# Log-sum-exp of 16384 rows on one core: one-pass row sums on VectorE, the last three sums in PSUM, most logs ahead of the last load

## The chip, the core and the metric

One core of one Trainium2 chip. The metric is the device time of one execution in microseconds (us). The profile's span is about 1.9 us shorter than that time (161.4 against 163.31 before). ScalarE is ACT in the profile, VectorE is DVE, SP is the engine that issues the loads.

## The reference

```python
def setup_inputs():
    batch, seq, dim = 32, 512, 1024
    return {"x": np.random.randn(batch, seq, dim).astype(np.float32), "axis": -1}

def reference(x, axis):
    x_max = np.max(x, axis=axis, keepdims=True)
    return (x_max.squeeze(axis) + np.log(np.sum(np.exp(x - x_max), axis=axis))).astype(np.float32)
```

The kernels take exp without subtracting the maximum, and were found correct in every run below.

## The kernel before

Each of the 128 partitions holds 128 rows of 1024 numbers. They come in 17 loads, into a ring of 51 rows. Per load, `(r, n_dve)` says: r rows, of which ScalarE takes the exp of the first `n_dve` in one instruction and VectorE sums them; of the others ScalarE takes exp and sum in one instruction per row. "A row" below is such a row on all partitions, 0.524 MB.

```python
CHUNKS = [
    (4, 1), (15, 11), (16, 10), (16, 15), (16, 0), (14, 0), (12, 9), (9, 5), (7, 5), (5, 4),
    (4, 3), (3, 0), (2, 2), (2, 2), (1, 0), (1, 0), (1, 0),
]
LN_AT = 5
# ... cut: ring, sums, res in SBUF; a semaphore per load; load(i) waits until its ring rows are free
    for i, (r, n_dve) in enumerate(CHUNKS):
        if i:
            load(i)
        s, row = place[i]
        if i == LN_AT:
            logged = row
            take_logs(0, logged, *done_before[i])      # waits for all sums of the loads before
        nc.scalar.wait_ge(landed[i], 16)
        if n_dve:
            nc.scalar.activation(out=ring[:, s : s + n_dve], in_=ring[:, s : s + n_dve],
                                 func=Exp).then_inc(act_done, 1)
            acts += 1
            nc.vector.wait_ge(act_done, acts)
            nc.vector.reduce_sum(out=sums[:, row : row + n_dve], in_=ring[:, s : s + n_dve],
                                 axis=AX).then_inc(dve_done, 1)
            # ... cut: bookkeeping
        for j in range(n_dve, r):
            nc.scalar.activation(out=ring[:, s + j], in_=ring[:, s + j], func=Exp,
                                 accum_out=sums[:, row + j : row + j + 1]).then_inc(act_done, 1)
            # ... cut
    take_logs(logged, NB, dves, acts)
    nc.scalar.dma_start(out=out_v, in_=res).then_inc(stored, 16)
```

The softmax here doesn't subtract the row's maximum and nothing guards it: scores larger than these inputs give would overflow.

## Time and profile before

| | before |
|---|---|
| time, median of 6 runs | 163.32 us (163.15 to 164.0) |
| span of the profiled run | 161.4 us |
| input queue's share of 16 DMA engines | 97.0% |
| last row landed / its exp started | 158.21 / 158.34 |

### The profile page before, as it was taken

To read this page: it belongs to the slowest core of one execution; us is meant where nothing else is said; L and a number is where in the kernel's file an instruction comes from. 1 tells how busy PE (TensorE), PEld (TensorE's weight loads), DVE (VectorE), ACT (ScalarE), POOL (GpSimd) and SP (SyncE) were. 2 spreads that over 40 slices of the span, in tenths; PEclk is the share of its full clock that TensorE was granted. 3 is DMA by queue.
4 is the path that set the end of the run, shared out by engine and by line. 5 is a ranking of instruction groups with operands and counts; after the bars stand their busy time and mean duration, and the time that the engine had idled before them with its cause. 6 is when DMAs were issued, how large, how long until landed. Compare 5 with 4: busy or idle time off the path is not lost.

```text
span 161.4 us, 212 instructions
## 1 busy us (share of the span) xinstructions
DVE 72.9 (45%) x11; ACT 124.1 (77%) x136; POOL 0.2 (0%) x4
## 2 busy tenths in 40 slices
DVE  0030000029960699000799920000004999799874
ACT  3190006997089980999429999999999999999995
POOL 0000000000000000000000000000000000000000
DMA  7999799989989989989989999999899999999990
GB/s 264 499 487 442 335 442 520 422 357 520 422 357 520 422 357 520 422 357 520 422 353 426 457 455 422 390 463 475 347 439 434 433 441 402 431 418 416 420 394 24
DMA packets 2593, 67.18 MB, mean 416 GB/s; under 512 B 288, under 2 KB 416, under 8 KB 800
## 3 DMA queue, kind: packets, MB, share of 16 engines
q1 hardware_dynamic: 2448, 67.11, 97.0%
q10 hardware_dynamic: 144, 0.07, 0.1%
q14 instruction: 1, 0.01, 0.0%
HBM read 67.11 MB, written 0.07 MB: 416 GB/s over the span
## 4 chain that ended last, share of the span: by engine, by line
ACT 52%; DMA 38%; DVE 7%; issue 1%
DMA ring<-in_x_dram 38%; ACT ring L127 30%; ACT ring L115 22%; DVE sums L120 7%; ACT res L92 0%
## 5 line engine op out<-in xcount | busy, mean ns | idle before, releaser
L120 DVE TENSOR_REDUCE sums<-ring 128x5 f32<-128x5120 f32 (+8 forms) x11 | 72.9, 6648 | 86.1 <-ACT ring L115 86.0
L115 ACT ACTIVATE ring<-ring 128x5120 f32<-128x5120 f32 (+8 forms) x11 | 59.3, 5395 | 29.6 <-DMA ring<-in_x_dram 29.6
L127 ACT ACTIVATE ring<-ring 128x1024 f32<-128x1024 f32 x61 | 63.4, 1041 | 5.3 <-DMA ring<-in_x_dram 5.3
L127 ACT ACTIVATION_READ_ACCUMULATOR ring<-ring 128x1 f32 x61 | 11.4, 187 | 0.0
L102 ACT ACT_TABLE_LOAD x1 | 1.3, 1283 | 0.8 <-PEq L181 0.8
L92 ACT ACTIVATE res<-sums 128x67 f32<-128x67 f32 (+1 forms) x2 | 0.5, 256 | 0.1
L181 POOL MEMSET const-bfloat16-1.0<- 128x1 bf16 x1 | 0.1, 101 | 0.0
L181 POOL MEMSET const-uint8-127<- 128x1 uint8 x1 | 0.1, 101 | 0.0
L181 POOL MEMSET const-float32-0.0<- 128x1 f32 x1 | 0.1, 98 | 0.2 <-issue 0.2
L181 POOL MEMSET const-float32-1.0<- 128x1 f32 x1 | 0.1, 98 | 0.0
## 6 DMA issues: line engine op xcount, KB each, us to landing
ring<-in_x_dram SPq DMA_DIRECT2D x1, 7680.0 KB, 24.9
ring<-in_x_dram SPq DMA_DIRECT2D x1, 7168.0 KB, 36.0
ring<-in_x_dram SPq DMA_DIRECT2D x1, 6144.0 KB, 21.6
ring<-in_x_dram SPq DMA_DIRECT2D x1, 4608.0 KB, 32.1
ring<-in_x_dram SPq DMA_DIRECT2D x2, 2048.0 KB, 26.3
ring<-in_x_dram SPq DMA_DIRECT2D x1, 3584.0 KB, 40.2
ring<-in_x_dram SPq DMA_DIRECT2D x1, 2560.0 KB, 44.4
ring<-in_x_dram SPq DMA_DIRECT2D x2, 1024.0 KB, 46.0
```

What stands on the lines that cost most here:

```text
L92: nc.scalar.activation(out=res[:, lo:hi], in_=sums[:, lo:hi], func=Ln).then_inc(act_done, 1)
L102: nc.scalar.preload_act_table_set("natural_log_exp_and_others")
L115: nc.scalar.activation(out=ring[:, s : s + n_dve], in_=ring[:, s : s + n_dve], func=Exp).then_inc(act_done, 1)
L120: nc.vector.reduce_sum(out=sums[:, row : row + n_dve], in_=ring[:, s : s + n_dve], axis=AX).then_inc(dve_done, 1)
L127: nc.scalar.activation(out=ring[:, s + j], in_=ring[:, s + j], func=Exp, accum_out=sums[:, row + j : row + j + 1],).then_inc(act_done, 1)
L181: nc = _bacc.Bacc("TRN2", target_bir_lowering=False, num_devices=1)
```

## The change

The intent: sum a row on VectorE in one pass of 512 columns, adding its two halves and accumulating (`tensor_tensor_reduce`), in place of a reduce over 1024; give VectorE 96 rows instead of 67; keep the sums of the last three rows in PSUM; and take all other logs before the last row, while ScalarE waits for it, so that only a log of three columns is left behind the last exp.

```diff
 CHUNKS = [
-    (4, 1), (15, 11), (16, 10), (16, 15), (16, 0), (14, 0), (12, 9), (9, 5), (7, 5), (5, 4),
-    (4, 3), (3, 0), (2, 2), (2, 2), (1, 0), (1, 0), (1, 0),
+    (4, 4), (15, 13), (15, 14), (16, 9), (16, 11), (16, 11), (12, 7), (9, 9), (7, 6),
+    (5, 3), (4, 3), (3, 3), (2, 2), (1, 1), (1, 0), (1, 0), (1, 0),
 ]
-LN_AT = 5
+LN_AT = 7
+LATE = 3
 # ... cut
+    late = nc.alloc_psum_tensor("late", [P, 512], fp32).ap()
 # ... cut: take_logs gets its source; total(t) is late[...] for the last three rows, else sums[...]
+        if i == len(CHUNKS) - 1:
+            take_logs(logged, late_row, sums[:, logged:late_row], *done_before[-LATE])
         nc.scalar.wait_ge(landed[i], 16)
 # ... cut
-            nc.vector.reduce_sum(
-                out=sums[:, row : row + n_dve], in_=ring[:, s : s + n_dve], axis=AX
-            ).then_inc(dve_done, 1)
+            for j in range(n_dve):
+                nc.vector.tensor_tensor_reduce(
+                    out=ring[:, s + j, : D // 2],
+                    in0=ring[:, s + j, : D // 2], in1=ring[:, s + j, D // 2 :],
+                    scale=1.0, scalar=0.0, op0=Add, op1=Add,
+                    accum_out=sums[:, row + j : row + j + 1],
+                ).then_inc(dve_done, 1)
 # ... cut
-                accum_out=sums[:, row + j : row + j + 1],
+                accum_out=total(row + j),
 # ... cut
-    take_logs(logged, NB, dves, acts)
+    take_logs(late_row, NB, late[:, : NB - late_row], dves, acts)
```

More of the change, by code (lines that the diff above doesn't have):

```diff
@@ L40 @@
     Ln = mybir.ActivationFunctionType.Ln
-    AX = mybir.AxisListType.X
+    Add = mybir.AluOpType.add
     x_v = x_flat.rearrange("(p t) d -> p t d", p=P)
@@ L86, in load, with take_logs @@
         )
-    def take_logs(lo, hi, dve_wait, act_wait):
+    def take_logs(lo, hi, src, dve_wait, act_wait):
         nonlocal acts
@@ L91, in take_logs, with total @@
         nc.scalar.wait_ge(dve_done, dve_wait)
-        nc.scalar.activation(out=res[:, lo:hi], in_=sums[:, lo:hi], func=Ln).then_inc(
-            act_done, 1
-        )
+        nc.scalar.activation(out=res[:, lo:hi], in_=src, func=Ln).then_inc(act_done, 1)
         acts += 1
+    late_row = place[-LATE][1]
+    assert not any(n_dve for _, n_dve in CHUNKS[-LATE:])
+    def total(t):
+        return late[:, t - late_row : t - late_row + 1] if t >= late_row else sums[:, t : t + 1]
     body = nc.main_func.blocks[-1]
@@ L111 @@
             logged = row
-            take_logs(0, logged, *done_before[i])
+            take_logs(0, logged, sums[:, :logged], *done_before[i])
+        if i == len(CHUNKS) - 1:
+            take_logs(logged, late_row, sums[:, logged:late_row], *done_before[-LATE])
         nc.scalar.wait_ge(landed[i], 16)
@@ L119 @@
             nc.vector.wait_ge(act_done, acts)
-            nc.vector.reduce_sum(
-                out=sums[:, row : row + n_dve], in_=ring[:, s : s + n_dve], axis=AX
-            ).then_inc(dve_done, 1)
-            dves += 1
             for j in range(n_dve):
+                nc.vector.tensor_tensor_reduce(
+                    out=ring[:, s + j, : D // 2],
+                    in0=ring[:, s + j, : D // 2],
+                    in1=ring[:, s + j, D // 2 :],
+                    scale=1.0,
+                    scalar=0.0,
+                    op0=Add,
+                    op1=Add,
+                    accum_out=sums[:, row + j : row + j + 1],
+                ).then_inc(dve_done, 1)
+                dves += 1
                 busy[s + j] = (0, dves)
```

## The prediction

> **What bounds the kernel now.** I read the page first, then the stretches of time, the groups by shape, and the instructions in order of time. Busy shares alone mislead: ScalarE (ACT) has 77% and VectorE (DVE) 45%, while the input's queue fills the span.
>
> ```profile
> span 161.4 us, 212 instructions
> DVE 72.9 (45%) x11; ACT 124.1 (77%) x136; POOL 0.2 (0%) x4
> ...
> q1 hardware_dynamic: 2448, 67.11, 97.0%
> ...
> ACT 52%; DMA 38%; DVE 7%; issue 1%
> ```
>
> The third line is the input: 67.11 MB, and its packets take 97% of what sixteen DMA engines have. The last line, the chain that ended last, seems to say otherwise (ACT 52%). The stretches of time settle it: columns are the stretch, DVE busy, ACT busy, POOL busy, clock, DMA share, GB/s.
>
> ```profile
> 10.00:15.00 5.00, 0.00 (x0) 1.71 (x4) 0.00 (x0) 1.00 0.91 393
> 15.00:20.00 5.00, 0.00 (x0) 0.00 (x0) 0.00 (x0) 1.00 0.94 406
> ...
> 64.50:83.84 19.34, 6.54 (x2) 14.04 (x4) 0.00 (x0) 1.00 0.99 427
> 83.84:100.00 16.16, 9.85 (x1) 16.16 (x31) 0.00 (x0) 1.00 0.98 425
> ...
> 155.00:156.00 1.00, 1.00 (x1) 1.00 (x1) 0.00 (x0) 1.00 1.02 406
> 156.00:157.00 1.00, 1.00 (x2) 1.00 (x2) 0.00 (x0) 1.00 1.01 406
> 157.00:158.00 1.00, 1.00 (x1) 1.00 (x3) 0.00 (x0) 1.00 0.32 127
> 158.00:159.00 1.00, 1.00 (x1) 1.00 (x3) 0.00 (x0) 1.00 0.00 0
> ```
>
> The stream never pauses, whether the engines rest or work, and its bytes end at about 157.3. The semaphore records of the loads (in the trace; no line of the page has them) give the time at which each load is whole: 67 rows at 83.84, 81 at 100.79, 93 at 115.32, 102 at 126.26, 109 at 134.80, 114 at 140.88, 118 at 145.77, 121 at 149.46, 123 at 151.96, 125 at 154.44, 126 at 155.73, 127 at 157.01, and all 128 at 158.24. So a row (0.524 MB) comes every 1.21 us, up to 1.29 in the short loads at the end. Beside 158.24 stands the tail of ScalarE, in order of time (start, duration):
>
> ```profile
> 158.34 1.04 ACT L127 ACTIVATE ring<-ring 128x1024 f32<-128x1024 f32 x1
> 159.28 0.19 ACT L127 ACTIVATION_READ_ACCUMULATOR ring<-ring 128x1 f32 x1
> 159.50 0.25 ACT L92 ACTIVATE res<-sums 128x61 f32<-128x61 f32 x1
> 159.78 0.37 ACTq L139 DMA_DIRECT2D out_dram<-res  x1
> ```
>
> This decides the case. ScalarE has been busy without a break since 83.84, and so owns the chain, but it starts the last row only 0.10 us after that row landed. Were ScalarE infinitely early, 0.10 us would be won. Behind it come 1.13 (exp and accumulator read), 0.03, 0.25 (log), 0.03 and 1.61 us (store). Times reported are about 1.9 us above the span (163.31 against 161.4).
>
> **The durations I shall use**, from the groups by shape (busy, mean ns of one):
>
> ```profile
> L120 DVE TENSOR_REDUCE sums<-ring 128x15 f32<-128x15360 f32 x1 | 16.2, 16153 | 12.8 <-ACT ring L115 12.8
> L120 DVE TENSOR_REDUCE sums<-ring 128x2 f32<-128x2048 f32 x2 | 4.5, 2282 | 2.0 <-ACT ring L115 2.0
> L115 ACT ACTIVATE ring<-ring 128x5120 f32<-128x5120 f32 x2 | 8.9, 4470 | 0.0
> ```
>
> A reduce of n rows: (16.153 - 2.282)/13 = 1.067 us per row plus 0.15, i.e. 1.042 ns per element. An exp over n rows without sums: successive starts in the timeline give 9.50 us for 11 rows, 4.38 for 5, 3.51 for 4, which is 0.853n + 0.10. An exp with its own sum: 1.04 per row from start to start. Thus a row summed by VectorE saves ScalarE 0.19 us, less 0.10 per batch.
>
> [...]
>
> **The change, part by part.**
>
> *One-pass sums.* Per row 512 columns of two streams in place of 1024 of one: 512 x 1.042 = 0.53 us[...]: estimate 0.72 us per row (0.61 to 0.85) against 1.08. With 96 rows in place of 67, VectorE is busy about 96 x 0.72 = 69 us against 72.9. Not a bound by itself.
>
> *ScalarE's work.* Before, 67 rows at 0.853, 11 batches at 0.10, 61 rows at 1.04: 121.7 us. After, 96 at 0.853, 14 at 0.10, 32 at 1.04: 116.6. So 5.1 us less. But the stream is not touched (17 loads as before, same order, same bytes), so most of that becomes waiting in the first 100 us.
>
> *Ring.* The loads reuse rows later freed by other engines. By the walk below the last load needs the second row of the 12-row load, summed by VectorE at about 124, then queues for 34 us; before it was issued at 112.5. The stream stays fed.
>
> *The end, walked.* Landings after the change are those above moved by one row where the cuts differ: 82 rows at 102.0, 94 at 116.5, 103 at 127.5, 110 at 136.0, 115 at 142.1, 119 at 147.0, 122 at 150.7, 124 at 153.2, then as before. ScalarE:
> - 16 rows (11 by VectorE): start 102.0, 9.49 + 5.20, free 116.7.
> - 12 rows (7): 6.07 + 5.20, free 128.0; then the first log, about 0.2: 128.2.
> - 9 rows (9): 7.78, free 135.9; waits for 136.0. 7 rows (6): 5.22 + 1.04, free 142.3. 5 rows (3): 2.66 + 2.08, free 147.0. 4 rows (3): 2.66 + 1.04, free 150.7. So it runs level with the stream.
> - 3 rows: 153.4. 2 rows: 155.2. Then 0.96 (one row, VectorE sums it): 156.15. Two rows with PSUM sums: 158.24. The second log, 31 columns: about 0.2, hidden only if ScalarE is early. By my count it is not: last row starts at 158.4, later than 158.34.
> - Tail: 1.13 + 0.03 + log of 3 columns, 0.253 - 58 x 0.83 ns = 0.20, + 0.03: store at 159.8, against 159.78.[...]
>
> *Sum:* +0.1 (last row later), -0.05 (short log)[...]: nothing, within 0.2 us. Span about 161.3, time 163.2.
>
> **Rivals.**
> 1. *ScalarE really is early*, as the change intends: the last row starts at 158.26 (landing plus 0.02), the second log hides. Saves 0.08 + 0.05[...]: 163.1. No way to more: the landing is the floor.
> 2. *The first log waits for VectorE.* It needs all seven sums of the 12-row load, begun at 122.8 when their exp ends: done at 122.8 + 7d. ScalarE asks at 128.0, so d over 0.74 makes it wait: d = 0.85 gives 128.8, 0.8 us lost, and the walk shows almost no slack to win it back: 164.0. My d of 0.72 is next to this threshold, so it is the likelier loss.
> 3. *Half rate.* d about 1.2 us: 11 sums from 111.6 end at 124.8, seven more at 133.2; ScalarE loses 5 us at the first log. Behind it the 27 further sums begin at 141 and end near 173.5; the end then hangs on VectorE: about 177 to 178 in time, 9% slower. Against it: the wish to give 96 rows to VectorE suggests a measured rate well under a row's 1.21 us.
> 4. *More SBUF traffic slows the loads.* The stream shows 393 to 406 GB/s with idle engines and 425 to 427 with both busy, so no.
>
> **Range and chances.** Faster by 2% would need 160.0, a span of 158.1, before the last row has even landed: only a faster stream could do it, 0.01. Slower by 2% needs 3.3 us, d of about 1.0 or more: 0.04. Most weight lies at 163.0 to 163.4, with a tail to 164.2 for rival 2; the runs before themselves spread from 163.25 to 164.0.
>
> **What would show it.** Right: load queue near 97%, last landing at 158.2 +- 0.2, one row's sum of about 0.7 us on VectorE with an accumulator read, ScalarE idle some 5 us more, all before about 102; last exp within 0.3 us of the landing. Rival 2: ScalarE idle before the first log, released by VectorE. Rival 3: a sum of 1.1 us or more. Wrong altogether: a last landing more than 1 us from 158.2, which nothing above foresees.

What no trace of this case shows is cut from the text above, and marked: one section, two terms of a one-pass sum's duration, and the term for PSUM in three places. With the cut terms the duration came to 0.72 us (0.61 to 0.85). From the trace alone, 512 columns at the reduce's 1.042 ns and its fixed 0.15 are an estimated 0.68, on the same side of rival 2's threshold of 0.74. That a pass over two streams keeps the reduce's rate was the author's assumption; no trace before the result showed it. Half that rate, rival 3, is a supposition too: 2 x 0.53 + 0.15 is about 1.2. The sum at the end came to "nothing, within 0.2 us" with the term for PSUM; the two terms that are left, +0.1 and -0.05, come to nothing as well. Rival 1's 163.1 had it too; what is left of its saving, 0.13 us, gives 163.2.

## More of the kernel before

One more line of the page before, from its list of DMA queues (packets, MB, share), matters in the end, and I read past it:

```profile
q14 instruction: 1, 0.01, 0.0%
```

This is a queue that the kernel doesn't issue to; the profile calls its kind "instruction", and the padded runs below show that it brings an engine its instructions (180 memsets more on VectorE, and it has 3 packets; 320 more, and it has 4). One packet, 8192 bytes, a rounding error by volume.

Two kinds of reading below come from the trace's records and are on no line of the page: the sixteen increments of each load's semaphore, one per DMA engine (the last of them is when the load is whole), and single DMA packets with start and duration. They stand in ordinary fences or tables, and each is from the one profiled run of its kernel.

## The result, and the profile after

164.34 us median of 6 runs (164.15 to 164.68) against 163.32: ratio 1.0061, 95% interval 1.0041 to 1.0080. Ratios here are the mean time of one kernel's fast runs over that of the other's of the same rounds, so not quite the ratio of the quoted medians. All runs were fast. All outputs are right. It is one microsecond slower, clear of noise, and above all that I gave weight to (163.0 to 163.4, with a tail to 164.2).

The page of the kernel after: span, busy shares, the instruction queue, the chain that ended last by engine, and the two groups of a one-pass sum:

```profile
span 162.4 us, 340 instructions
...
DVE 59.7 (37%) x192; ACT 119.0 (73%) x82; POOL 0.2 (0%) x4
...
q14 instruction: 3, 0.02, 0.0%
...
DMA 70%; ACT 18%; DVE 9%; issue 1%; SPq 0%
...
L131 DVE CUSTOM_DVE_ANT_0 ring<-ring 128x512 f32<-128x512 f32 x96 | 59.6, 687 | 98.8 <-ACT ring L125 98.8
...
L131 DVE DVE_READ_ACCUMULATOR2_ANT sums<- 128x1 f32 x96 | 7.9, 82 | 0.0
```

Everything that the change meant to do, it did. VectorE has 29 more rows and less work. A sum is 0.69 us and its accumulator read lies beside the next sum. The chain is now the loads' (70%) where it was ScalarE's (52%). The tail of ScalarE after, in order of time:

```profile
158.34 1.04 ACT L144 ACTIVATE ring<-ring 128x1024 f32<-128x1024 f32 x1
159.29 0.16 ACT L144 ACTIVATION_READ_ACCUMULATOR ring<-ring 128x1 f32 x1
159.34 0.22 ACT L96 ACTIVATE res<-sums 128x31 f32<-128x31 f32 x1
159.46 1.06 ACT L144 ACTIVATE ring<-ring 128x1024 f32<-128x1024 f32 x1
160.42 0.15 ACT L144 ACTIVATION_READ_ACCUMULATOR ring<-ring 128x1 f32 x1
160.61 0.17 ACT L96 ACTIVATE res<-late 128x3 f32<-128x3 f32 x1
160.81 0.37 ACTq L156 DMA_DIRECT2D out_dram<-res  x1
```

The second log is out of the way before the last row starts, the last log takes 0.17 in place of 0.25, and from the last exp to the store it is 160.81 - 159.46 = 1.35 us where it was 159.78 - 158.34 = 1.44. But the last exp starts at 159.46, for its row is whole at 159.44, 1.23 us later than before. So: +1.23 (landing), -0.10 (ScalarE 0.02 behind the landing, not 0.12), -0.10 (shorter tail, 0.096 before rounding): +1.03, which is the store's 160.81 - 159.78.

Why is the row late? The stretches of time (stretch, DVE, ACT, POOL, clock, DMA share, GB/s) of the kernel after, to hold against the prediction's lines of the same stretches:

```profile
157.00:158.00 1.00, 1.00 (x5) 1.00 (x2) 0.00 (x0) 1.00 0.44 176
158.00:159.00 1.00, 0.49 (x2) 1.00 (x3) 0.00 (x0) 1.00 0.06 25
```

0.06 is one engine of sixteen. Before, the stretch from 158 to 159 had nothing; after, one DMA engine alone is still moving bytes. The semaphore increments say the same; each pair is the slowest DMA engine and the next to it:

| rows whole | before | after |
|---|---|---|
| 118, after 119 | 145.74, 145.74 | 147.24, 147.08 |
| 121, after 122 | 149.44, 149.42 | 151.91, 150.77 |
| 128 | 158.21, 158.20 | 159.44, 158.33 |

Fifteen engines finish after the change within 0.13 us of when they did before (158.33 against 158.20). One loses 0.98 us between 147.24 and 151.91 (4.67 us, where the next takes 3.69) and never gets it back: each engine brings one increment of every load, and the slowest two are 1.14 us apart at 151.91 and still 1.11 at 159.44. The DMA packets around there (start, end, queue, bytes):

```
149.288 149.753 q1  12288
149.381 149.846 q1  12288
149.536 149.860 q14 8192      <- instructions
149.848 150.968 q1  12288     <- 1.12 us where the others take 0.46
149.860 150.325 q1  12288
```

An instruction fetch, and right behind it the one load packet that takes 1.12 us.

### The profile page after: what moved, and what is told of

Read it like the earlier page. It is cut to its first block, busy times and chain, and to the rows that moved or that the text cites. A ratio compares the mean times of both kernels' runs of the same rounds, so it can differ in the third digit from the quotient of the medians.

```text
span 162.4 us, 340 instructions
## 1 busy us (share of the span) xinstructions
DVE 59.7 (37%) x192; ACT 119.0 (73%) x82; POOL 0.2 (0%) x4
## 4 chain that ended last, share of the span: by engine, by line
DMA 70%; ACT 18%; DVE 9%; issue 1%; SPq 0%
DMA ring<-in_x_dram 70%; ACT ring L125 17%; DVE ring L131 9%; ACT ring L144 1%; SPq L88 0%; DVE sums L131 0%; ACT res L96 0%
## 5 line engine op out<-in xcount | busy, mean ns | idle before, releaser
L125 ACT ACTIVATE ring<-ring 128x3072 f32<-128x3072 f32 (+9 forms) x14 | 84.4, 6046 | 40.9 <-DMA ring<-in_x_dram 40.9
L131 DVE CUSTOM_DVE_ANT_0 ring<-ring 128x512 f32<-128x512 f32 x96 | 59.6, 687 | 98.8 <-ACT ring L125 98.8
L144 ACT ACTIVATE ring<-ring 128x1024 f32<-128x1024 f32 x32 | 33.2, 1041 | 0.0
L131 DVE DVE_READ_ACCUMULATOR2_ANT sums<- 128x1 f32 x96 | 7.9, 82 | 0.0
L144 ACT ACTIVATION_READ_ACCUMULATOR ring<-ring 128x1 f32 x32 | 5.9, 184 | 0.0
L96 ACT ACTIVATE res<-sums 128x94 f32<-128x94 f32 (+1 forms) x2 | 0.5, 253 | 0.0
```

The costliest lines, as they stand in the source:

```text
L96: nc.scalar.activation(out=res[:, lo:hi], in_=src, func=Ln).then_inc(act_done, 1)
L131: nc.vector.tensor_tensor_reduce(out=ring[:, s + j, : D // 2], in0=ring[:, s + j, : D // 2], in1=ring[:, s + j, D // 2 :], scale=1.0, scal ...
```

## The experiments

**Theory F.** VectorE's program is 198 instructions long in the trace where it was 17 (each one-pass sum is two instructions). It is fetched in pieces by a DMA engine that also carries the load, and each fetch sets that engine's share of the loads back, so that it ends behind the others: a straggler. In the trace of the change 55 VectorE instructions have started by the first fetch and 176 by the second, 121 apart, so a piece of 8192 bytes is an estimated 121 instructions. **Rival T:** the one-pass sums read two streams and write one, and this traffic disturbs the loads near the end. **Rival F-late:** fetches hurt only among the short loads of the end, so it is when, not how many.

| kernel | median us | ratio to before (95%) | VectorE fetches at | last row whole, slowest engine / next |
|---|---|---|---|---|
| before | 163.32 | | none | 158.21 / 158.20 |
| the change | 164.34 | 1.0061 (1.0041 to 1.0080) | 62.3, 149.5 | 159.44 / 158.33 |
| a1_early_reduce | 163.51 | 1.0004 (0.9991 to 1.0016) | 76.8 | 158.57 / 158.23 |
| a2_early_pad | 164.35 | 1.0052 (1.0040 to 1.0065) | 6.5, 77.4 | 159.25 / 158.47 |
| b1_pad180 | 164.64 | 1.0071 (1.0058 to 1.0083) | 15.8, 98.6 | 159.56 / 158.56 |
| b2_pad320 | 165.49 | 1.0122 (1.0106 to 1.0137) | 15.7, 59.5, 101.6 | 160.41 / 158.37 |
| c1_tail_alone | 164.27 | 1.0052 (1.0039 to 1.0065) | none | 158.32 / 158.17 |
| d1_one_pass_end_only | 163.36 | 0.9996 (0.9982 to 1.0011) | none | 158.38 / 158.16 |
| d2_last_cuts | 164.01 | 1.0043 (1.0023 to 1.0063) | none | 158.35 / 158.14 |
| d3_level | 163.31 | 0.9990 (0.9976 to 1.0003) | none | 158.47 / 158.23 |

(In the experiments' rounds, before was 163.35 to 163.45.) Every kernel also has one fetch that I give to ScalarE: it comes at 89 to 90 with the program that ScalarE had before (146 instructions in the trace), at 132 with the change's (93), and doesn't move when only VectorE's program is padded. VectorE's are those that do move. The four kernels with no fetch for VectorE behind before (c1, d1, d2, d3) have their last row whole at 158.32 to 158.47, so a difference of 0.2 us in this column from one kernel to another says nothing.

### a1_early_reduce: fewer VectorE instructions, the end untouched

```diff
+            if i < 2:
+                nc.vector.reduce_sum(out=sums[:, row : row + n_dve], in_=ring[:, s : s + n_dve], axis=AX).then_inc(dve_done, 1)
+                ...
+            else:
                 for j in range(n_dve):
                     nc.vector.tensor_tensor_reduce(...)
```

> The change, with the sums of the first two loads (17 rows) taken by two TENSOR_REDUCEs as before: 160 VectorE instructions for the sums in place of 192. In the trace of the change one DMA engine of sixteen ends its share of the 3-row load 0.98 us behind, right after an 8192-byte packet of the instruction queue at 149.54; the other fifteen are as before. Theory F (VectorE's longer program is fetched by the DMA engines that carry the load; the second fetch makes a straggler): no fetch near 149.5, no straggler, the last load whole at 158.2 to 158.6, time 163.0 to 163.4, 1.0 us below the change. Rival T (the two-stream sums disturb the loads near the end by their SBUF traffic): the last 79 sums are unchanged, so the last load is whole at 159.4 and the time stays at 164.3.

Measured: 163.51, no fetch near 149.5, no straggler; last row whole at 158.57. 0.11 us above the range I wrote for F, which the one remaining fetch at 76.8 explains in part (the slowest engine is 0.34 behind the next, and was 0.36 behind from 83 us on). The last 79 one-pass sums ran as in the change, so T falls: 32 instructions in the first 45 us decide 0.83 us at the end.

### a2_early_pad: the same number of fetches, earlier

```diff
+    for k in range(100):
+        nc.vector.memset(pad[:, k : k + 1], 0.0)
     logged = 0
```

> The change, with 100 one-column memsets on VectorE before its first sum, so that its program is 100 instructions longer and each fetch comes earlier: I expect the fetches of its queue in the first 10 us and near 80 us, and none after 130 from VectorE. Theory F by number (every fetch costs the same one DMA engine's share some 0.6 to 1.0 us, whenever it falls, since each engine has its fixed part of every load): two fetches still, the last load whole near 159.4, time 164.0 to 164.6. Rival F-late (only a fetch among the short loads of the end hurts): last load whole at 158.3, time 163.1 to 163.4. Rival T: 164.3.

Measured: 164.35, as the change. The fetches moved to 6.5 and 77.4, and the straggler with them: by the load that is whole after 77.4 the slowest engine is 0.79 us behind the next (83.72 against 82.93), and it is 0.78 behind at the end. F-late falls: what a DMA engine loses at 77 us it still lacks at 159.

### b1_pad180 and b2_pad320: the kernel before with nothing but more instructions

```diff
             dves += 1
+            if i < 4:
+                for k in range(45 * i, 45 * i + 45):          # b2: 80
+                    nc.vector.memset(pad[:, k : k + 1], 0.0)
```

> The kernel before, with 45 one-column memsets on VectorE after each of its first four reduces: 180 more instructions, no other change; VectorE is idle there. Theory F by number: two fetches for VectorE in the first 110 us, one DMA engine about 1 us behind, last load whole at 159.0 to 159.5, time 164.0 to 164.6. Rival F-late and rival T: 163.3 as before, since nothing happens near the end and no sum has changed.

> As the last, with 80 memsets after each of the four reduces (320 in all): three fetches for VectorE. Theory F by number: one more step of 0.6 to 1.0 us, last load whole near 160.2, time 164.8 to 165.5. Rivals F-late and T: 163.3.

Measured: 164.64 (0.04 above the range) and 165.49 (in it). VectorE was idle where the memsets ran, and no sum, cut or log differs from before. The page of b2: span, VectorE's and the instruction queue's lines.

```profile
span 163.6 us, 532 instructions
...
DVE 79.3 (48%) x331; ACT 124.0 (76%) x136; POOL 0.2 (0%) x4
...
q14 instruction: 4, 0.03, 0.0%
```

320 memsets add 6.4 us to VectorE's busy time, none of it on the path; three more packets of 8192 bytes move the end by 2 us. The slowest engine of b2 against the median of the sixteen, load by load: across the fetch at 59.5 it takes 20.31 us for a load where the median takes 19.41 (0.90 lost), across that at 101.6 17.96 against 16.97 (0.99). In b1, across 98.6: 17.90 against 16.94 (0.96). The change across 149.5, against its median: 4.67 against 3.71 (0.96). That is four times nearly the same price. The memsets' own writes are no rival: b1's last block of them runs from 94.08 to 94.74, and the one packet that is drawn out is the one behind the fetch at 98.6 (2.78 us where others of its size take 2.12).

The losses of one run add up on one DMA engine: in b2 it is 0.43, 1.35 and 2.11 us behind the next slowest after its three fetches, at the loads whole at 45.45, 65.76 and 103.07. The packets say so directly: on one engine a packet starts within 0.02 us of the end of the one before, so they can be chained, into sixteen chains. All three VectorE fetches of b2 lie on one chain, as do both of b1 and both of the change; ScalarE's fetch lies on another. The first fetch costs the kernel less than the later ones, since the sixteen end 0.8 us apart anyway (157.40 to 158.21 before) and only the slowest counts: one fetch (a1) moved the last landing by 0.36 us (only 0.10 past the latest run without one), two by 1.0 to 1.35, three by 2.2.

### c1_tail_alone: the change's end on the kernel before

```diff
+LATE = 3
+    late = nc.alloc_psum_tensor("late", [P, 512], fp32).ap()
+        if i == len(CHUNKS) - 1:
+            take_logs(logged, late_row, sums[:, logged:late_row], *done_before[-LATE])
-                accum_out=sums[:, row + j : row + j + 1],
+                accum_out=total(row + j),
-    take_logs(logged, NB, dves, acts)
+    take_logs(late_row, NB, late[:, : NB - late_row], dves, acts)
```

> The kernel before with the tail of the change alone: the last three rows' sums in PSUM, the logs of all other rows taken ahead of the last row, the log of three rows at the end; TENSOR_REDUCE and cuts as before. What is at stake is what the tail is worth without the one-pass sums. I expect the second log to wait for VectorE: its last reduce ended at 159.01 before, where ScalarE asks at about 158.3. So the last exp starts near 159.15 in place of 158.34, the end behind it is 0.09 us shorter (1.35 from start to store in the change against 1.44): 0.7 us slower than before, 163.9 to 164.3, ScalarE idle 0.7 us released by VectorE. No fetch for VectorE, last load whole at 158.2. If instead the tail is worth its 0.1 us alone: 163.3.

Measured: 164.27, as written (the last exp starts at 159.38, a little later than the 159.15 expected). The waits of c1 (who waited for whom, us in total, times, longest), and its end in order of time:

```profile
ACT res L96 <- DVE sums L132: 0.7, 1, 0.7
```

```profile
158.31 0.16 ACT L139 ACTIVATION_READ_ACCUMULATOR ring<-ring 128x1 f32 x1
159.22 0.25 ACT L96 ACTIVATE res<-sums 128x58 f32<-128x58 f32 x1 [0.74 <-DVE sums L132]
159.38 1.04 ACT L139 ACTIVATE ring<-ring 128x1024 f32<-128x1024 f32 x1
```

The early log needs VectorE's last sums, and with reduces these come 0.74 us too late. So the two halves of the change need each other: the tail needs the one-pass sums near the end, but only there.

### d1, d2, d3: one-pass sums only where they are needed

d1 is c1 with one-pass sums from the tenth load on (14 rows, 35 instructions for all sums) and the 3-row load given to VectorE:

```diff
-    (4, 3), (3, 0), (2, 2), (2, 2), (1, 0), (1, 0), (1, 0),
+    (4, 3), (3, 3), (2, 2), (2, 2), (1, 0), (1, 0), (1, 0),
+ONE_PASS_FROM = 9
+            if i < ONE_PASS_FROM:
                 nc.vector.reduce_sum(...)
+            else:
+                for j in range(n_dve): nc.vector.tensor_tensor_reduce(...)
```

> The kernel before with the tail of the change, one-pass sums for its loads from the tenth on only (14 rows, 28 instructions), and the 3-row load given to VectorE: 35 VectorE instructions for all sums, under the 46 or so after which the padded runs show the first fetch. Theory F: no fetch for VectorE, all sixteen DMA engines whole at 158.2 to 158.4; the one-pass sums end by 157.7, so the second log does not wait; the last exp starts at 158.25 to 158.45 and the end is 0.09 us shorter: 163.2 to 163.4 where the kernel before has 163.45 in the last runs, a gain of 0 to 0.2 us. Rival: if one-pass sums near the end disturb the loads after all (theory T), last load whole at 159 or later and 164 or more.

Measured: 163.36. No fetch for VectorE, last row whole at 158.38, no wait for VectorE. ScalarE, not being early, starts the last exp at 158.59, 0.21 behind the landing.

```diff
-    (16, 0), (14, 0), (12, 9), (9, 5), (7, 5), (5, 4), (4, 3), (3, 3), (2, 2), (2, 2), (1, 0), ...   d1
+    (16, 0), (15, 0), (12, 9), (9, 5), (7, 5), (5, 4), (4, 4), (3, 3), (2, 2), (1, 1), (1, 0), ...   d2
```

> The version d1_one_pass_end_only with the change's cuts at the end (one row more in the sixth load, two single-row loads fewer rows to wait for: 2, 1, 1, 1, 1) and all four rows of the 4-row load given to VectorE. In d1 ScalarE was bound by its own chain from the landing of 125 rows on, so the second log delayed the last row by 0.15 to 0.2 us (158.59 against a landing of 158.38). Here by the same durations it ends the last but one row at about 158.0 to 158.1, so the second log hides: last exp within 0.05 us of the landing at 158.2 to 158.4, no fetch for VectorE (35 instructions), time 163.1 to 163.3, 0.15 to 0.3 us below before (163.45 in the last runs). If the chain is longer than I count, 163.3 to 163.5 as d1.

Measured: 164.01, a miss. The loads were fine (158.35); the fault was in my arrangement. ScalarE waits 1.33 us for the longer sixth load, takes it row by row, and is behind from there on: the last exp starts at 159.18.

```diff
-    (16, 0), (15, 0), (12, 9), (9, 5), (7, 5), (5, 4), ...   d2
+    (16, 0), (15, 11), (12, 9), (9, 5), (7, 5), (5, 5), ...   d3
```

> d2_last_cuts with its fault mended: there ScalarE waited 1.33 us for the 15-row load and then took it row by row (15 x 1.04 us), and never caught up (last exp at 159.18, landing 158.35). Here VectorE sums 11 rows of that load and all five of the 5-row load, which takes about 2 us off ScalarE's chain. By the durations of the trace ScalarE then meets the stream at 116.7, 127.6, 136.1, 142.4 and 147.1 and ends the last but one row at about 158.05: last exp within 0.1 us of the landing at 158.25 to 158.4, end 1.34 us behind it. 38 VectorE instructions for sums, no fetch. Time 163.2 to 163.4 against 163.4 for before: at most 0.2 us better, since nothing can start before the last row has landed. If it is 163.5 or more, ScalarE's chain is still the bound, and its wait for the last load will be absent.

Measured: 163.31 against 163.35. The end of d3:

```profile
158.31 0.25 ACT L97 ACTIVATE res<-sums 128x58 f32<-128x58 f32 x1
158.50 1.06 ACT L155 ACTIVATE ring<-ring 128x1024 f32<-128x1024 f32 x1
159.46 0.15 ACT L155 ACTIVATION_READ_ACCUMULATOR ring<-ring 128x1 f32 x1
159.64 0.17 ACT L97 ACTIVATE res<-late 128x3 f32<-128x3 f32 x1
159.84 0.37 ACTq L167 DMA_DIRECT2D out_dram<-res  x1
```

Here everything that the change wanted is in place: the last exp starts 0.02 us after its row (158.47), the log is hidden, and 1.34 us later the store is issued. It equals the kernel before within the interval (0.9976 to 1.0003), as the prediction's arithmetic of the end said: there was only 0.10 + 0.10 us to win, and a landing 0.1 to 0.3 us later than in the profiled run of before takes that away. No version here beats the kernel before clearly.

## Why the prediction was wrong

- **The step that failed:** "But the stream is not touched (17 loads as before, same order, same bytes)". The bytes of the loads are the same, but the stream also carries instructions. The term that I sized at 0 measured +1.23 us on the last landing. Of this, 1.11 is one engine behind the other fifteen (159.44 against 158.33), and 0.98 of it came at the fetch at 149.5. The first fetch, at 62.3, prepared it: that engine was 0.83 us ahead of the slowest, lost 0.85 (0.31 for the fetch, and 2.96 us for the next packet where the others take 2.42), and was level with the slowest from there on, so that it had no slack when the second came. The remaining 0.12, by which the other fifteen are late too, is open; the kernels without a VectorE fetch differ by up to 0.26 us among themselves (158.21 to 158.47).
- **Two readings of the trace were off, without effect on the result:** the landings by 0.03 us (the last row's exp starts 0.12 us behind its landing, not 0.10), and the end of the stream's bytes, "about 157.3": the last packet ends at 157.78.
- **"The last load whole at 158.2 +- 0.2"** was my own test for the steps, and "more than 1 us from 158.2, which nothing above foresees" is what came. Rival 4 asked whether more SBUF traffic slows the loads and answered no. That answer stands (one-pass sums up to the end, and the last row whole at 158.57 in a1, 158.38 in d1, 158.47 in d3); the question was too narrow.
- **Durations of the new sums: right.** Estimated 0.72 us a row from start to start (0.61 to 0.85), measured 0.61: the instruction is 0.687 us, as 0.53 + 0.15 from the reduce's rate and fixed part, and the accumulator read (0.082) overlaps the next sum (both start at 112.55). Rival 3 (half rate) is refuted: at half the reduce's rate the 512 columns alone would take 1.07 us, and the whole instruction takes 0.687.
- **Rival 2 (the first log waits for VectorE): didn't happen.** The last sum of the 12-row load ended at 127.57, the log started at 128.40, right behind ScalarE's own last accumulator read at 128.18.
- **ScalarE's walk: right to 0.4 us where the landings were right.** Predicted free at 116.7 and 128.2 after the first log; measured 117.01 and 128.58. It met the stream from there on, as computed.
- **The second log hidden or not:** I counted it as not hidden. In the change it is hidden (last exp 0.02 behind the landing), with the last row 1.23 us late. In d1, where the row is whole at 158.38, it delays the last row, as I counted; d3 shows that other cuts hide it (0.02).
- **The tail: right.** -0.05 for the short log predicted, and a term for PSUM that is cut; -0.10 in all measured, the low end of both together: the log takes 0.17 in place of 0.25, and an accumulator read of ScalarE 0.15 to 0.16 into PSUM where it takes 0.18 to 0.19 into SBUF.
- **The chances:** 0.95 on "within 2%" holds; the tail to 164.2 missed by 0.14 us, for want of the one term.

What stays open: the fetch packet itself takes 0.31 to 0.33 us, and the engine loses 0.85 to 0.99. The trace shows the rest in the load packet next to it (1.12 us in place of 0.46), not why.

## What to carry to other kernels

When a kernel is bound by a stream that all DMA engines share evenly, the slowest engine sets the end (here 159.44, with the next at 158.33), so look at the spread of a load's completions, not only at the mean rate: a straggler of 1 us shows as a DMA share of 0.06 in the last stretch. In such a kernel the number of instructions is a cost of its own, even on an idle engine (1.2 us for b1's 180 memsets, 2.0 for b2's 320). It comes in steps: 24 to 27 more VectorE instructions (d1 to d3) brought no fetch, 180 more (b1) brought two. So compare program lengths before and after, and use a finer-grained operation only where its latency is on the path (14 rows here), not on all 96. And before working to make an engine earlier that is 0.12 us behind the last landing, note that 0.12 us is the whole prize for that.
